# Two query columns of the linear memory moved into a seven-product unit, two heads' delays changed, first weights in two transfers

## The chip, the cores and the metric

The kernel runs on one core of one Trainium2 chip. The metric is device time in microseconds (us) for one launch, the median of repeated runs. The profile is one further execution, recorded instruction by instruction. Its engines are PE (matrix products), ACT and DVE (element-wise work, ACT with function tables), POOL (element-wise work and DMAs that accumulate) and SP (DMA issues). PEld is the weight load that belongs to each matmul.

## The reference

One layer of a streaming encoder on 512 prompt tokens and 64 tokens of a running stream, width 1024, in float32:

```python
h = layer_norm(ALPHA * x + 0.5 * swiglu_ffn(x, ffn1_w_gu, ffn1_w_down))
q, k, v, o, i, f, a_q, a_k, a_v, g_ml, g_att = split(h @ w_in)
qk, new_conv = silu(causal_dwconv(concat([q, k]))), last 3 rows of (history, q, k)
# linear memory ("mLSTM"): 4 heads of 256, chunked, with states C, n, m
y_ml  = (norm(mlstm(q, k / 16, v, i, f)) * g * sigmoid(o)) @ w_ml_proj
y_att = band_attention(a_q, a_k, a_v) @ w_att_proj          # 16 heads of 64
h = layer_norm(ALPHA * h + (sigmoid(g_ml) * y_ml + sigmoid(g_att) * y_att) @ w_out)
y = layer_norm(ALPHA * h + 0.5 * swiglu_ffn(h, ffn2_w_gu, ffn2_w_down))
```

`w_in` is a block of 1024-row columns of 128 outputs each: columns 0 to 7 are q of the linear memory (two for each head: 0 and 1 for head 0, 4 and 5 for head 2), 8 to 15 its k, 16 to 23 v, 24 to 31 o; 32 to 55 are attention q, k, v, and 56 to 71 the two gates. The queries and keys of the linear memory pass a causal convolution over four tokens and a SiLU before they are used.

## The kernel before

All activations lie feature-major, 128 features by 576 tokens a tile. Each float32 operand is split in a high part and a low remainder (`wh`, `wl` for weights; hi, lo for activations), and each product is three matmuls: wh·hi, wh·lo, wl·hi. ACT makes `wh` and DVE `wl`; for the columns in the set `ADDED`, `wl` comes instead from ACT (the negated high part) and an accumulating POOL DMA that reads the weights again.

The stages, by the times of the profile: the first feed-forward block until about 405 us; the columns of `w_in` for v, o, most gates and attention v as *units* (about 435 to 585 us); attention with its q and k columns (until about 780); the attention projection (until 850); the linear memory, heads 0 to 3 (850 to about 1043); two projections; the second feed-forward block (1160 to 1548).

Two kinds of product occur. A plain column (`gemm`) takes 8 feature tiles by 3 matmuls by two halves of the tokens, 256 and 320 wide: 48 matmuls. A unit (`Units`, `Columns`) makes a 2-by-2 block, two columns by two halves of 288 tokens, in seven products rather than eight (the Strassen-Winograd scheme): 7 products by 4 feature tiles by 3 matmuls are 84 matmuls, 288 wide. It needs sums of weight tiles on DVE and ACT, and sums of activation tiles (`Combos`), made once in each stage that has units: `Combos.make` splits eight sums, each with the hi part on ACT and the lo part as an ACT pass (times -1) and an accumulating POOL DMA (`add_lo`). `Columns` writes the outputs to two tiles of 576 tokens, and a `keep` function stores these off chip.

The order on PE is written by hand. `od.now` is a clock that each matmul moves on by a nominal time; `later(dt, fn)` puts a piece of work on a heap, and `od.tick()`, called between feature tiles of the plain columns, places each piece that has come due between them. The orders of ACT, DVE, POOL and SP are set by the framework's scheduler from priorities and dependences. Every engine runs its list in order.

In the linear memory a head has these pieces. `ml_kq`: two k columns, then two q columns; `conv_start` copies a column's result out of its bank to the tile `R` on ACT, `conv_rest` runs four DVE passes over `R` to `U`, SiLU on ACT to `qf` and the split (`qk` for the queries). `turn5` turns keys (`qf`) and values (`vf`, loaded from off chip) by five transposes; the sinks write `kwh`, `vh` on ACT and `kwl`, `vl` on DVE. `ml_decay` makes `Mb` and the decay tiles `D` by Exp on ACT; SiLU and Exp lie in different function tables, so an ACT_TABLE_LOAD stands before each change. `weights(b)` multiplies q with k (`aux<-qk,s`) and scales by `D` to `W`; `state(e)` multiplies k with v (`aux<-vh,kwh`) to `cn`, `cs`; `hidden(b)` multiplies `W` with v (`aux<-vh,W`). Each of these pieces has its own delay after the head's k or q columns. The pieces of a head come due during the columns of the next.

At the start eight transfers are under way at once; later ones wait for one of them. The first three weight columns come in k-pairs of feature tiles: gate 0 and gate 1 in one transfer, up 0 in another. `ones_r` is a constant made on ACT.

Of the kernel before, what the change touches and what calls it, by code (L numbers as in the profile page):

```python
# [17 lines left out]
P = 128  # L18
# [68 lines left out]
def tile_layer(ctx: ExitStack, tc: tile.TileContext, ins, outs):  # L87
# [37 lines left out]
    def f(ap):  # L125
        return ap.bitcast(F32)
# [305 lines left out]
    def plan_in(cols_):  # L432
        for c in cols_:
            plan.append((("in", c), w_in[c]))
# [10 lines left out]
        a, b = ins["w_ap"][j], ins["w_ap"][j + 1]  # L445
        plan += [(("dsap", j, x), w) for x, w in (("a", a), ("u", b), ("t", None), ("b", b[:, :512]))]
    for h in range(4):
        plan_in((8 + 2 * h, 9 + 2 * h, 2 * h, 2 * h + 1, *FILL[h]))
    plan_in((63,))
    plan += [(("mp", j), ins["w_mp"][j]) for j in range(KT)]  # L450
    plan += [(("o", j), ins["w_o"][j]) for j in range(KT)]
# [19 lines left out]

    for k0 in range(0, KT, 2):
        ww = slice(k0 * P, (k0 + 2) * P)
        SP.dma_start(w0[:, 0:3:2, ww], ins["w_gu1"][0:2, :, ww].rearrange("c p n -> p c n"))
        load_x(0, k0, ACT if k0 < 4 else SP)
        SP.dma_start(w0[:, 1, ww], ins["w_gu1"][FT, :, ww])
    for k0 in range(0, KT, 2):
        load_x(1, k0, SP)
    cols = const.tile([P, NCOL], F32, name="cols")
# [38 lines left out]
                    prev = split_x(0, k0 + c)  # L518
    for k in range(KT):
        split_x(1, k)  # L520
    act(ones_r, one_, scale=1.0 / P)
    first.close()


# [246 lines left out]
    class Combos:  # L771
# [876 lines left out]
    KEEP = {48: keep_a, 16: keep_v, 24: keep_o, 56: keep_g, 64: keep_g}  # L1648
    pairs = [(c, b) for c in range(0, KT, 2) for b in (16, 24)] + [(0, 56), (6, 64), (2, 48), (4, 48), (6, 48)]
# [178 lines left out]
    hp = hstack.enter_context(tc.tile_pool(name="hp", bufs=8, reuse_waits="tile"))  # L1828
    HF = []
    mstack = ExitStack()  # L1830
    mp = mstack.enter_context(tc.tile_pool(name="ml", bufs=1, reuse_waits="tile"))
    conv_st = mp.tile([P, 16, 6], F32, name="conv_st")
    vh, vl = (mp.tile([P, 5, 258], F32R, name=s) for s in ("vh", "vl"))
# [32 lines left out]
    def conv_rest(ct, scale, room, tail=None):  # L1866
# [31 lines left out]
    hid, states, backs, order = [0], [0], [0], {}  # L1898

    def ml_kq(h):  # L1900

# [18 lines left out]
        for e in range(2):  # L1920
# [9 lines left out]
            def v_turn(vf, sink):  # L1930

                if hid[0] < 5 * h:
                    later(300, lambda: v_turn(vf, sink))
                else:
                    turn5(vf, sink)

            later(7500 + 6500 * e, lambda vf=vf, s=v_sink, fn=v_turn: fn(vf, s))
        ml_decay(h, st)
        qtail = mp.tile([P, 2, NS], F32, tag="qtail", name=nm("qtail"))
        for e in range(2):  # L1940
            ct = 2 * h + e
            cb = conv_start(ct)
            gemm(one(("in", ct)), H, [cb])
            _, hi, lo = conv_rest(ct, 1.0, lambda: slot(F32R, mp, "qk", bufs=4), qtail[:, e, :])
            st["q"].append((hi, lo))
        st["qtail"] = qtail
        return st

# [39 lines left out]
    def ml_early(h, st):  # L1988
# [33 lines left out]

        for b in range(5):

            later(10000 + 2100 * b if h == 3 else 11000 + 2600 * b, lambda b=b: weights(b))

    def ml_late(h, st):
        W, (c0, ch, cl), wdb, qs_ = st["W"], st["C"], st["wdb"], st["qs"]
# [20 lines left out]

        def hidden(b):  # L2050

            assert backs[0] == 2 * h
            ps = bank()
            if b < 4:
                w = P
# [226 lines left out]
```

## Time and profile before

| what | value |
|---|---|
| three runs | 1551.35, 1549.96 and 1551.93 us, median 1551.35 |
| the profiled execution | 1550.32 us, its span 1548.6 us, granted clock 0.999 |
| PE busy in the span | 1532.1 us, 99% |
| DVE, ACT, POOL busy | 1163.7 us (75%), 884.1 us (57%), 198.5 us (13%) |

The 1.7 us between the profiled time and its span lie before the first and after the last instruction. Times of the trace count from the span's start. A row of the timeline gives start, duration, engine, line, operation, tiles written and read, shape and count, and in brackets the idle time before it with what ended it. Rows of one form that follow each other are put together; their durations then overlap, since the engines start an instruction before the last has left. So what one instruction costs in a queue is the distance from its start to the next one's start. The 48 matmuls of a plain column write a bank named `mm`, attention and memory pieces a bank named `aux`.

### The profile page before, as it was taken

The numbers are of one execution on the slowest core, as the hardware profiler recorded it, in microseconds if no ns is written. First come the engines' busy times: TensorE is split into PE (matmuls) and PEld (weight loads), VectorE is DVE, ScalarE is ACT, GpSimd is POOL, SyncE is SP. The second block draws the span as 40 slices with busy tenths as digits, with TensorE's granted clock in tenths as the row PEclk, the third lists the DMA queues.
The fourth block names the chain that finished last, engine by engine and source line by source line (L and its number), as shares of the span: only waits on it lengthen the run. The fifth ranks groups of instructions, "written<-read, shape, count | busy, mean of one in ns | idle before, by whom it ended". The sixth has DMA issues, their size and how long they took to land.

```text
span 1548.6 us, 29509 instructions
## 1 busy us (share of the span) xinstructions
PE 1532.1 (99%) x11587; PEld 1516.3 (98%) x11587; DVE 1163.7 (75%) x2256; ACT 884.1 (57%) x1672; POOL 198.5 (13%) x372
## 2 busy tenths in 40 slices
PE   9999999999999999999999999999999999999998
PEld 9999999999999999999999999999999999999997
DVE  7877778756999767887677577765779878787756
ACT  7545446533766557776864777753456454557323
POOL 2000000100200015544300311102120000001000
PEclk9999999999999999999999999999999999999999
DMA  9322223534544448676634965542653323217244
GB/s 258 113 100 92 94 98 103 129 107 148 174 149 147 151 171 228 160 181 156 141 99 146 278 147 138 121 141 83 200 122 104 109 82 110 82 64 192 81 128 150
DMA packets 80259, 211.93 MB, mean 137 GB/s; under 512 B 9080, under 2 KB 20984, under 8 KB 80120
## 3 DMA queue, kind: packets, MB, share of 16 engines
q1 hardware_dynamic: 66072, 172.29, 33.9%
q0 software_dynamic: 12896, 36.05, 13.3%
q8 instruction: 91, 1.49, 0.4%
q10 hardware_dynamic: 1152, 1.70, 0.3%
q14 instruction: 48, 0.39, 0.1%
HBM read 174.82 MB, written 22.22 MB: 127 GB/s over the span
## 4 chain that ended last, share of the span: by engine, by line
PE 45%; DVE 3%; ACT 3%; issue 1%; DMA 0%; POOL 0%; DVEq 0%; ACTq 0%; POOLq 0%
PE mm L133 35%; PE aux L133 8%; PE aux L143 1%; DVE U L153 1%; DVE s L153 1%; ACT L147 0%; DMA wr<-in_w_ap 0%; ACT wh L147 0%; ACT sc L147 0%; DVE o L150 0%; DVE wl L150 0%; DVE s L150 0%; ACT R L147 0%; ACT qf L147 0%; ACT s L147 0%
## 5 line engine op out<-in xcount | busy, mean ns | idle before, releaser
L133 PE MATMUL mm<-s,wh 128*128 128x288 f32 (+2 forms) x3430 | 700.9, 298 | 1.1 <-DVE s L150 0.4
L133 PEld LDWEIGHTS mm<-s,wh 128*128 128x128 f32 x3430 | 548.7, 189 | 4.2 <-DVE s L150 1.5
L133 PE MATMUL mm<-s,wl 128*128 128x288 f32 (+2 forms) x1705 | 503.2, 295 | 0.0
L133 PEld LDWEIGHTS mm<-s,wl 128*128 128x128 f32 x1705 | 321.1, 188 | 0.2 <-DVE wl L150 0.2
L147 ACT ACTIVATE wh<-wr 128x1024 fp32r<-128x1024 f32 (+2 forms) x136 | 133.0, 979 | 144.6 <-PE mm L133 85.5
L133 PE MATMUL mm<-tx,wh 128*128 128x288 f32 x778 | 158.4, 296 | 0.0
L150 DVE TENSOR_TENSOR wl<-wr,wh 128x1024 fp32r<-128x1024 f32 (+2 forms) x97 | 108.8, 1125 | 56.9 <-ACT wh L147 56.8
L133 PEld LDWEIGHTS mm<-tx,wh 128*128 128x128 f32 x778 | 124.9, 188 | 0.0
L133 PE MATMUL mm<-tx,wl 128*128 128x288 f32 x383 | 113.0, 295 | 0.6 <-DVE wl L150 0.6
L916 ACT ACTIVATE wh<-wt 128x1024 fp32r<-128x1024 f32 x53 | 56.2, 1060 | 88.4 <-DVE wt L150 88.4
L150 DVE TENSOR_TENSOR wl<-wt,wh 128x1024 fp32r<-128x1024 f32 x53 | 64.8, 1222 | 53.9 <-ACT wh L916 52.7
L133 PE MATMUL mm<-h,wh 128*128 128x256 f32 (+2 forms) x384 | 78.3, 295 | 0.0
L150 DVE TENSOR_TENSOR wl<-wu,wh 128x1024 fp32r<-128x1024 f32 x50 | 61.2, 1223 | 22.1 <-ACT wh L916 22.1
L197 POOL DMA_DIRECT2D s<-s x16 | 13.7, 855 | 491.4 <-ACT s L147 252.2
L133 PEld LDWEIGHTS mm<-tx,wl 128*128 128x128 f32 x383 | 72.0, 188 | 0.9 <-DVE wl L150 0.9
L916 ACT ACTIVATE wh<-wu 128x1024 fp32r<-128x1024 f32 x50 | 52.9, 1058 | 32.7 <-PE mm L133 32.5
L147 ACT ACTIVATE h<-h 128x288 f32<-128x288 f32 x80 | 35.0, 437 | 64.1 <-DVE h L150 64.0
L150 DVE TENSOR_TENSOR wl<-ws,wh 128x1024 fp32r<-128x1024 f32 x53 | 64.6, 1219 | 0.4 <-ACT wh L916 0.3
L150 DVE TENSOR_TENSOR ws<-wu 128x1024 f32<-128x1024 f32 x53 | 64.3, 1214 | 0.0
L133 PEld LDWEIGHTS mm<-h,wh 128*128 128x128 f32 x384 | 61.5, 188 | 0.2
L916 ACT ACTIVATE ah<-wu 128x512 fp32r<-128x512 f32 x53 | 33.4, 631 | 44.6 <-PE mm L133 41.3
L133 PE MATMUL mm<-h,wl 128*128 128x256 f32 (+2 forms) x192 | 56.5, 294 | 0.0
(397 smaller groups left out, 3622.0 us busy)
## 6 DMA issues: line engine op xcount, KB each, us to landing
wu<-in_w_gu SPq DMA_DIRECT2D x80, 512.0 KB, 4.3
wr<-in_w_in SPq DMA_DIRECT2D x46, 512.0 KB, 4.1
wr<-in_w_dn SPq DMA_DIRECT2D x40, 512.0 KB, 3.5
wl<-in_w_in POOLq DMA_DIRECT2D x38, 512.0 KB, 7.0
wu<-in_w_in SPq DMA_DIRECT2D x26, 512.0 KB, 4.5
wr<-in_w_dn SPq DMA_DIRECT2D x20, 384.0 KB, 3.4
s<-s POOLq DMA_DIRECT2D x16, 288.0 KB, 3.6
wr<-in_w_ap SPq DMA_DIRECT2D x8, 512.0 KB, 3.5
```

What stands on the lines that cost most here:

```text
L133: PE.matmul(out, lhsT, rhs, start=start, stop=stop, **kw)
L143: PE.transpose(out, in_, idn)
L147: return ACT.activation(out, in_, func, **kw)
L150: return (eng or DVE).tensor_tensor(out, a, b, op=op)
L153: return DVE.scalar_tensor_tensor(out=out, in0=a, scalar=s, in1=b, op0=op0, op1=op1)
L197: return POOL.dma_start(lo, src, accum_op=ALU.add)
L916: self.last = ACT.activation(hi, src, AF.Copy)
```

## The change

1. **A fourteenth unit.** Columns 1 and 5 (the second query column of heads 0 and 2) become one unit behind the thirteen. `keep_q` stores its two tiles off chip (`QD`). Heads 0 and 2 no longer have these two plain columns: three remain in each.
2. **The pieces of heads 0 and 2.** `conv_load` fetches the stored column into a tile `RQ` by two SP transfers and makes the two small POOL copies; the rest of the convolution runs on `RQ` rather than `R`, 1000 nominal ns after the decays. The delays of heads 0 and 2 change: the second turn of v from 14000 to 12000, `weights` from 11000 + 2600b to 13000 + 2600b, `state` from 5500 + 1800e to 9000 + 1800e, `hidden` from 19500 + 2200b to 21000 + 2200b. `state` is put back by 300 while not both turns of v have been placed.
3. **The start.** The first k-pair of gate 0 and gate 1 comes in two transfers, gate 0 first, then up 0, then gate 1. `ones_r` is made behind the splits of the first tokens.
4. **`Combos.make`.** Of the eight lo parts, those of n = 0 with i = 2, 3 are a DVE subtraction rather than ACT and a POOL DMA.

```diff
-        plan_in((8 + 2 * h, 9 + 2 * h, 2 * h, 2 * h + 1, *FILL[h]))
+        plan_in((8 + 2 * h, 9 + 2 * h, 2 * h, *((2 * h + 1,) if h in (1, 3) else ()), *FILL[h]))
...
-        SP.dma_start(w0[:, 0:3:2, ww], ins["w_gu1"][0:2, :, ww].rearrange("c p n -> p c n"))
+        if k0:
+            SP.dma_start(w0[:, 0:3:2, ww], ins["w_gu1"][0:2, :, ww].rearrange("c p n -> p c n"))
+        else:
+            SP.dma_start(w0[:, 0, ww], ins["w_gu1"][0, :, ww])
         load_x(0, k0, ACT if k0 < 4 else SP)
         SP.dma_start(w0[:, 1, ww], ins["w_gu1"][FT, :, ww])
+        if not k0:
+            SP.dma_start(w0[:, 2, ww], ins["w_gu1"][1, :, ww])
...
-    act(ones_r, one_, scale=1.0 / P)
+    with tc.issue_after(prev.ins):
+        act(ones_r, one_, scale=1.0 / P)
...
-                        self.added = add_lo(lo, hi, t)
+                        if n or i < 2:
+                            add_lo(lo, hi, t)
+                        else:
+                            tt(lo, t, f(hi), ALU.subtract)
...
+    QD = {c: away("qd") for c in (1, 5)}
+
+    def keep_q(c, tiles):
+        for e in range(2):
+            SP.dma_start(QD[c + 4 * e], tiles[e])
...
-    pairs = [...] + [(0, 56), (6, 64), (2, 48), (4, 48), (6, 48)]
-    un = Columns([(b + c, b + c + 1) for c, b in pairs],
+    pairs = [...] + [(0, 56), (6, 64), (2, 48), (4, 48), (6, 48), (1, 0)]
+    un = Columns([(b + c, b + c + (1 if b else 4)) for c, b in pairs],
...
+    RQ = rqp.tile([P, LR], F32, name="RQ")
+    POOL.memset(RQ[:, 0:3], 0.0)
...
+    def conv_load(ct):
+        DVE.tensor_copy(RQ[:, 515:518], cols[:, C_HIST + 3 * ct:C_HIST + 3 * ct + 3])
+        SP.dma_start(RQ[:, 3:515], QD[ct][:, 0:NP_])
+        SP.dma_start(RQ[:, 518:582], QD[ct][:, NP_:])
+        POOL.tensor_copy(conv_st[:, ct, 0:3], RQ[:, 512:515])
+        POOL.tensor_copy(conv_st[:, ct, 3:6], RQ[:, 579:582])
...
-            later(7500 + 6500 * e, lambda vf=vf, s=v_sink, fn=v_turn: fn(vf, s))
+            later(7500 + (6500 if h in (1, 3) else 4500) * e, lambda vf=vf, s=v_sink, fn=v_turn: fn(vf, s))
...
-        for e in range(2):
+        if h in (0, 2):
+            conv_load(2 * h + 1)
+            later(1000, lambda: st.update(q1=conv_rest(2 * h + 1, 1.0, room, qtail[:, 1, :], RQ)[1:]))
+        for e in range(1 if h in (0, 2) else 2):
...
-            later(10000 + 2100 * b if h == 3 else 11000 + 2600 * b, lambda b=b: weights(b))
+            later(10000 + 2100 * b if h == 3 else (11000 if h == 1 else 13000) + 2600 * b, lambda b=b: weights(b))
...
         def state(e):
+            if vts[0] < 2 * h + 2:
+                later(300, lambda: state(e))
+                return
...
-            later(5500 + 1800 * e, lambda e=e: state(e))
+            later((5500 if h in (1, 3) else 9000) + 1800 * e, lambda e=e: state(e))
...
-            later(16000 + 1800 * b if h == 3 else 19500 + 2200 * b, lambda b=b: hidden(b))
+            later(16000 + 1800 * b if h == 3 else (19500 if h == 1 else 21000) + 2200 * b, lambda b=b: hidden(b))
```

Two places show what this does to the engines' lists. Both are ACT's. The first is the head of its list, behind its first four transfers (`w` is the tile of the first three weight columns, `s` on the right the raw tokens). Before:

```order
L147 ACT_TABLE_LOAD
L147 ACTIVATE ones_r<-one 128x128
L514 ACTIVATE wh_99<-w_90 128x256
L503 ACTIVATE s_71<-s_91 128x256
L514 ACTIVATE wh_101<-w_90 128x256
L503 ACTIVATE s_73<-s_92 128x256
L514 ACTIVATE wh_103<-w_90 128x256
```

And in the changed kernel:

```order
L519 ACT_TABLE_LOAD
L519 ACTIVATE wh_99<-w_90 128x256
L508 ACTIVATE s_71<-s_91 128x256
L519 ACTIVATE wh_101<-w_90 128x256
L508 ACTIVATE s_73<-s_92 128x256
L519 ACTIVATE wh_103<-w_90 128x256
```

The pass for `ones_r` is gone from ahead of the first weights; in SP's list the first transfer (128x2x256 before) is now 128x256, and every transfer from the second k-pair on stands one place later. The second place is its list in head 0 of the linear memory, around the second turn of v, whose result `vh` (128x4x128, then 64x128) the state products need. Before:

```order
L147 ACTIVATE kwh<-aux_11143,tcol 128x128
L147 ACTIVATE kwh<-aux_11156,tcol 64x128
L147 ACTIVATE wl_11194<-wh_11193 128x1024
L147 ACTIVATE R<-mm_11079 128x256
L147 ACTIVATE R<-mm_11126 128x256
L147 ACTIVATE R<-mm_11126 128x64
L147 ACTIVATE kwh<-aux_11143,tcol 128x128
L147 ACTIVATE vh<-aux_11200 128x4x128
L147 ACTIVATE vh<-aux_11207 64x128
L147 ACTIVATE kwh<-aux_11143,tcol 128x128
L147 ACT_TABLE_LOAD
L147 ACTIVATE qf_11074<-U_11069 128x512
```

And in the changed kernel, where the stored column's SiLU (`qf`) comes ahead and the first decays `D` stand between:

```order
L147 ACTIVATE vh<-aux_11255 64x128
L147 ACTIVATE qf_11128<-U_11123 128x512
L147 ACTIVATE qf_11128<-U_11123 128x64
L147 ACT_TABLE_LOAD
L147 ACTIVATE D_11194<-Mb_11088,tcol 64x64
L147 ACTIVATE qk_11129<-qf_11128 128x576
L147 ACTIVATE kwh<-aux_11295,tcol 128x128
L147 ACTIVATE kwh<-aux_11308,tcol 64x128
L147 ACTIVATE D_11197<-Mb_11088,tcol 128x512
L147 ACTIVATE kwh<-aux_11295,tcol 128x128
L147 ACTIVATE vh<-aux_11315 128x4x128
L147 ACTIVATE vh<-aux_11322 64x128
```

The second `vh` now stands behind the table load, two decays and the stored column's SiLU and split. On PE 39 matmuls of plain columns stood between the second turn of v and the first state product, and now 21; from the first state product to the first of `weights(0)` there were 51 matmuls, and now 42.

More of the change, by code (lines that the diff above doesn't have):

```diff
@@ L1646, in keep_a @@
             SP.dma_start(outs["v"][:, c + e, :], tiles[e])
-    KEEP = {48: keep_a, 16: keep_v, 24: keep_o, 56: keep_g, 64: keep_g}
-    pairs = [(c, b) for c in range(0, KT, 2) for b in (16, 24)] + [(0, 56), (6, 64), (2, 48), (4, 48), (6, 48)]
-    un = Columns([(b + c, b + c + 1) for c, b in pairs],
+    KEEP = {0: keep_q, 48: keep_a, 16: keep_v, 24: keep_o, 56: keep_g, 64: keep_g}
+    pairs = [(c, b) for c in range(0, KT, 2) for b in (16, 24)] + [(0, 56), (6, 64), (2, 48), (4, 48), (6, 48), (1, 0)]
+    un = Columns([(b + c, b + c + (1 if b else 4)) for c, b in pairs],
                  [lambda tiles, c=c, fn=KEEP[b]: fn(c, tiles) for c, b in pairs],
@@ L1830, in tile_layer @@
     mstack = ExitStack()
+    rqp = mstack.enter_context(tc.tile_pool(name="rq", bufs=1, side="right", reuse_waits="tile"))
     mp = mstack.enter_context(tc.tile_pool(name="ml", bufs=1, reuse_waits="tile"))
@@ L1864, in conv_start, with conv_rest @@
         return cb
-    def conv_rest(ct, scale, room, tail=None):
+    def conv_load(ct):
[4 more added lines that the diff above has]
+        POOL.tensor_copy(conv_st[:, ct, 3:6], RQ[:, 579:582])
+    def conv_rest(ct, scale, room, tail=None, R=R):
         U = mp.tile([P, LU], F32, tag="U", name=nm("U"))
@@ L1896, in turn5 @@
                 sink(b0, nb, w, ps[:w, :nb * P].rearrange("p (b c) -> p b c", c=P))
-    hid, states, backs, order = [0], [0], [0], {}
+    hid, states, backs, vts, order = [0], [0], [0], [0], {}
     def ml_kq(h):
@@ L1935, in v_turn @@
                     turn5(vf, sink)
-            later(7500 + 6500 * e, lambda vf=vf, s=v_sink, fn=v_turn: fn(vf, s))
+                    vts[0] += 1
+            later(7500 + (6500 if h in (1, 3) else 4500) * e, lambda vf=vf, s=v_sink, fn=v_turn: fn(vf, s))
         ml_decay(h, st)
         qtail = mp.tile([P, 2, NS], F32, tag="qtail", name=nm("qtail"))
-        for e in range(2):
+        room = lambda: slot(F32R, mp, "qk", bufs=4)
+        if h in (0, 2):
+            conv_load(2 * h + 1)
+            later(1000, lambda: st.update(q1=conv_rest(2 * h + 1, 1.0, room, qtail[:, 1, :], RQ)[1:]))
+        for e in range(1 if h in (0, 2) else 2):
             ct = 2 * h + e
@@ L1943, in ml_kq @@
             gemm(one(("in", ct)), H, [cb])
-            _, hi, lo = conv_rest(ct, 1.0, lambda: slot(F32R, mp, "qk", bufs=4), qtail[:, e, :])
-            st["q"].append((hi, lo))
+            st["q"].append(conv_rest(ct, 1.0, room, qtail[:, e, :])[1:])
+        if h in (0, 2):
+            st["q"].append(st["q1"])
         st["qtail"] = qtail
@@ L2050, in hidden @@
         def hidden(b):
-            assert backs[0] == 2 * h
+            assert backs[0] == 2 * h and vts[0] == 2 * h + 2
             ps = bank()
```

## The prediction

> **What bounds the kernel now.** I read the busy times of the page first, then the chain that ended last, then windows by stage, and last the timelines of the two places where the lists change.
>
> ```profile
> PE 1532.1 (99%) x11587; PEld 1516.3 (98%) x11587; DVE 1163.7 (75%) x2256; ACT 884.1 (57%) x1672; POOL 198.5 (13%) x372
> ```
>
> PE is the bound nearly everywhere: 16.5 us of the span of 1548.6 are all the idle time it has. So a change can win in two ways, fewer or shorter matmuls, or some of those gaps; and it can lose by new gaps. The chain in the second feed-forward stage, made of units alone, gives the price of a unit's matmul:
>
> ```profile
> 1198.22 201.08 PE mm L133 x1518
> ```
>
> That is 132.5 ns for each 288-wide matmul. The windows below hold the units of `w_in` (the first), the first two plain columns of the linear memory (the second: 96 matmuls of the columns, and two records at its edges), the pieces of head 0, and heads 1 to 3. The columns are the window, its length, the busy time with the count of PE, PEld, DVE, ACT and POOL, PE's granted clock, the DMA share and GB/s.
>
> ```profile
> 435.00:585.00 150.00, 149.21 (x1123) 148.44 (x1122) 122.10 (x170) 87.47 (x135) 7.73 (x11) 1.00 0.47 157
> 850.17:862.97 12.80, 12.80 (x98) 12.80 (x97) 4.50 (x11) 6.90 (x9) 6.35 (x19) 1.00 0.94 263
> 862.97:911.00 48.03, 47.63 (x363) 46.34 (x362) 32.55 (x74) 41.07 (x94) 10.10 (x25) 1.00 0.88 226
> 911.00:1043.00 132.00, 132.00 (x1024) 130.66 (x1023) 97.56 (x250) 90.54 (x203) 21.76 (x56) 1.00 0.53 134
> ```
>
> Two things are to be seen. Two plain columns cost 12.80 us without a gap. And in head 0 (third row) ACT is busy for 41.07 of 48.03 us, 86%, where in heads 1 to 3 it is 69%: head 0 is the one place of this stage where ACT is short of time, and it is the place whose list changes most.
>
> **The matmuls: -1.67.** The unit costs 84 x 132.5 ns = 11.13 us. The two plain columns that go cost 12.80 us. PE's own work falls by 1.67 us. The Trainium skill ("TensorE: Matmul & The Clock Gate", Back-to-back issue gap) gives N/2.4 + 2.5 ns for an isolated warm matmul. By that the saving would be estimated at 48 x (109.2 + 135.8) - 84 x 122.5 ns = 1.47 us; the rows give more for each matmul, and the measured ones stand in the sum.
>
> **The unit beside PE: 0 (0 to +0.5).** It brings the sums of weight tiles on DVE and ACT. The first window shows what covers them: about 13 units in 150 us with PE busy for 149.21, so DVE at 81% and ACT at 58% leave 0.79 us of idle time in all, 0.06 a unit. Its own work goes at that same rate. Its four weight tiles of 512 KB and the two stores of 288 KB meet a DMA share of 0.47. In exchange heads 0 and 2 lose their plain column's load, its accumulating transfer and its passes; each gains 288 KB of loads. In head 0 that relieves a DMA share of 0.88 to 0.94. I take 0; as upper bound, nearly the idle time of the whole window once more.
>
> **The start: -0.1, and `Combos.make`: -0.3 (together -0.7 to +0.5).** Timelines of ACT, PE and SP at the start, and the loads' sizes with the median time from issue to landing:
>
> ```profile
> 2.76 1.28 ACT L147 ACT_TABLE_LOAD   x1 [2.76 <-issue]
> 4.05 0.31 ACT L147 ACTIVATE ones_r<-one 128x128 fp32r<-128x128 f32 x1
> 4.31 0.42 ACT L514 ACTIVATE wh<-w 128x256 fp32r<-128x256 f32 x1
> 7.26 0.42 ACT L514 ACTIVATE wh<-w 128x256 fp32r<-128x256 f32 x1 [1.22 <-DMA w<-in_w_gu]
> 5.08 0.97 PE L133 MATMUL mm<-s,wh 128*128 128x256 f32 x2 [0.23 <-ACT s L503]
> 2.31 0.47 SPq L476 DMA_DIRECT2D w<-in_w_gu  x1
> 3.92 0.38 SPq L474 DMA_DIRECT2D w<-in_w_gu  x1
> w<-in_w_gu SPq DMA_DIRECT2D x4, 256.0 KB, 4.8
> ...
> w<-in_w_gu SPq DMA_DIRECT2D x4, 128.0 KB, 3.8
> ```
>
> Without `ones_r`, and with half the bytes in the first transfer, the first pass can start at 4.05 rather than 4.31, and PE's first product at 4.82 rather than 5.08. But at 7.26 ACT waited 1.22 us for the second k-pair of weights, and the bytes ahead of that pair are the same as before. PE then has 0.26 us more to wait there. So nearly all of it is given back; I keep 0.1. The bad end is the queue: SP stood still from 2.78 to 3.92, since a ninth transfer waits for one of the eight in flight. After the change the ninth is the second pair's up column (issued at 2.31 before), now at about 3.9. With 3.8 us to land it is there at 7.7, and ACT wants it behind the pass of 7.26, at about 7.9: 0.2 to spare.
>
> Later in the same stage the combined sums are made, and PE has one stall:
>
> ```profile
> 33.16 0.68 ACT L147 ACTIVATE s<-s 128x576 fp32r<-128x576 f32 x1
> 34.30 1.05 ACT L916 ACTIVATE wh<-wu 128x1024 fp32r<-128x1024 f32 x1
> 35.38 1.22 DVE L150 TENSOR_TENSOR wl<-wu,wh 128x1024 fp32r<-128x1024 f32 x1 [0.47 <-ACT wh L916]
> 36.66 0.40 PE L133 MATMUL aux<-s,wl 128*128 128x288 f32 x1 [0.73 <-DVE wl L150]
> ```
>
> PE waited 0.73 us for `wl`, which waited for ACT's `wh`, which stood behind the negating pass of 33.16 (0.68, of which about 0.1 overlaps the next). By the changed list that pass is one of those that go, and DVE gets a subtraction of 576 in its stead (0.76, by the 576-wide pass in the next fence). ACT brings `wh` about 0.6 earlier, but DVE has only its idle 0.47 there to take up the 0.76, so the new pass holds `wl` back by about 0.3: I take 0.3 back of the 0.73. In the other two stages that make such sums, PE shows no such wait, and I take nothing.
>
> **Head 0 of the linear memory: +2.3 (-0.6 to +4.5).** ACT, then DVE, then PE, around the second turn of v, the state products and `weights(0)`; the last row is `weights(0)` of head 1:
>
> ```profile
> 870.58 0.38 ACT L147 ACTIVATE R<-mm 128x256 f32<-128x256 f32 x1 [1.35 <-DVE U L153]
> ...
> 876.64 1.31 ACT L147 ACTIVATE D<-Mb,tcol 128x384 f32<-128x384 f32 x3
> 877.84 0.64 ACT L147 ACTIVATE ch<-c 128x516 fp32r<-128x516 f32 x1
> 878.37 1.06 ACT L147 ACTIVATE wh<-wr 128x1024 fp32r<-128x1024 f32 x1
> ...
> 880.76 0.77 ACT L147 ACTIVATE R<-mm 128x256 f32<-128x256 f32 x3
> 881.39 0.39 ACT L147 ACTIVATE kwh<-aux,tcol 128x128 fp32r<-128x128 f32 x1
> 881.63 0.78 ACT L147 ACTIVATE vh<-aux 128x512 fp32r<-128x512 f32 x2
> ...
> 882.68 1.28 ACT L147 ACT_TABLE_LOAD   x1
> 883.98 0.63 ACT L147 ACTIVATE qf<-U 128x512 f32<-128x512 f32 x1
> ...
> 889.23 0.77 ACT L147 ACTIVATE qf<-U 128x512 f32<-128x512 f32 x2
> 890.03 0.69 ACT L147 ACTIVATE qk<-qf 128x576 fp32r<-128x576 f32 x1
> 882.29 0.69 DVE L150 TENSOR_TENSOR vl<-aux,vh 128x512 fp32r<-128x512 f32 x1
> 890.75 0.76 DVE L153 SCALAR_TENSOR_TENSOR qk<-qf,qk 128x576 fp32r<-128x576 f32 x1 [0.19 <-ACT qk L147]
> 878.34 0.71 PE L143 MATMUL aux<-ident,vf 128*128 128x128 f32 x5
> 878.80 0.48 PE L133 MATMUL mm<-s,wh 128*128 128x256 f32 x2
> 884.03 0.28 PE L133 MATMUL aux<-vh,kwh 128*128 128x258 f32 x1
> 890.31 1.09 PE L133 MATMUL aux<-qk,s 128*128 128x512 f32 x4
> 891.57 0.73 PE L133 MATMUL aux<-qk,s 128*128 128x512 f32 x2 [0.16 <-DVE qk L153]
> 901.97 0.77 PE L143 MATMUL aux<-ident,qf 128*128 128x128 f32 x5 [0.19 <-ACT Mb L147]
> 932.20 1.57 PE L133 MATMUL aux<-qk,s 128*128 128x512 f32 x6
> ```
>
> Before, ACT worked without a pause from 870.58 to the second `vh` at 881.63: 28 instructions in 11.05 us. DVE's `vl` ended at 882.98, and the state products came at 884.03, so they had 1.05 us to spare. In the changed list 24 instructions stand between the same two points. Gone from there are three decays (1.20, to the start of `ch`), `ch` (0.53) and three `R` copies (0.63); new are the stored column's SiLU and split (about 0.7 and 0.6, from 889.23 and 890.03 less the overlap). That is 11.05 - 2.36 + 1.3 = 9.99 us, so `vh` starts at 880.57. `vl` starts 0.66 us behind it and takes 0.69: 881.9, and 882.1 if DVE has part of another pass before it.
>
> PE comes much earlier. Counted by its list, the second turn of v stands 1.24 us earlier, at 877.10. The turn takes 0.46, and the 21 matmuls that remain take 21 x 0.134 = 2.82 (39 of them took 5.23, from 878.80 to 884.03). So PE is at the first state product at 880.38, 3.65 earlier than before, where ACT is 1.06 earlier. It waits until 882.1: **+1.7**.
>
> `weights(0)` follows. 42 matmuls (30 of 0.12, 12 of 0.134) bring PE there at 887.3. The stored query column is the second that `weights(0)` reads; the plain one, which is late, is the first. Its split stands in ACT's list behind the last `vh`, three decays, two `kwh`, `ch`, three `R`, a table load, two SiLU passes and a `cn`, which add up to 5.75 us by the distances of their starts (the dearest in the rows above: 1.30 for the table load, 1.20 for the decays). So hi runs from 886.3 to 887.0, and DVE's lo takes 0.76, at once or behind up to 0.8 of a pass of the convolution: 887.8 to 888.6. The second matmul needs it. I take 888.5, near the late end, since DVE's row before shows such a pass ahead of the first lo: **+1.2**.
>
> Before, `weights(0)` took from 890.31 to 892.30, 1.99 us, where head 1's took 1.57; and PE lost 0.19 at 901.97. PE comes later to both pieces relative to what they wait for, and I count these 0.6 as gone: 1.7 + 1.2 - 0.6 = **+2.3**. The low end is that ACT and DVE clear both in time and the 0.6 go. The high end has 2.5 and 2.0 at the two places, and nothing gone.
>
> The rest costs nothing, each by a cover. The `RQ` transfers of head 0 are issued about 9 us ahead of the first pass over them, and loads took 3.8 to 4.8 us at the crowded start. POOL's two copies of head 2's `RQ` stand ahead of head 0's masks on `D`, which only `weights(0)` wants. Where `hidden` comes later, PE has columns to fill in. Heads 1 to 3 lose no time before (132.00 of 132.00 in the windows), and ACT at 69% there has room for head 2's moved pieces.
>
> **The sum.** -1.67 + 0 - 0.4 + 2.3 = +0.2 on the profiled 1550.32 us: 1550.5. That execution lies 1.03 below the median of the runs, so against the median I give **1551.5**: no change, since less than 0.2%, 3.1 us, can hardly be told from none here.
>
> **The rivals.**
> *The gain comes through.* ACT or DVE reach `vh` and the late query a good 2 us sooner than my sum, for instance since passes that I put in sequence overlap. For it: ACT's list there waited for nothing, so whatever it is spared shows at once. Then -1.67 - 0.4 + 0 = -2.1, 1549.3: still within 0.2%.
> *Faster.* The same, the old gaps go too (-0.6), and so does the whole stall ahead of 36.66 (-0.4 more): -3.1, 1548.2, just at the bound. Against it: it needs three covers to hold at once.
> *Slower.* One mechanism: the stored column's SiLU, its split and the table loads stand ahead of `vh` in ACT's in-order list, in head 2 as in head 0. If head 2 waits as head 0 does (2 x 2.3) and one of the two runs to the high end (+2.2), the sum is -2.1 + 6.8 = +4.7: 1556.1. It decides from 5.2 us of such waits. Against it: ACT at 69%, not 86%, behind head 0.
> *The split start loses.* A transfer of 128 KB that is issued into full queues takes longer than the 3.8 us; at 5.1 (the 256 KB ones took 4.8) the second pair's up column lands at 9.0, 1.1 us after ACT wants it: +1.1 instead of -0.1, so 1552.7. The Trainium skill ("DMA: Bandwidth & Descriptors", on measured sizes) has the rule to batch transfers to 1 MiB or more, as small ones carry a fixed cost; by that, splitting one of 256 KB is a loss. The row of 128 KB with 3.8 us, behind the 256 KB with 4.8, has the small one landing sooner, and that weakens it.
>
> **Chances.** The waits eat the gain: 0.46. The gain comes through: 0.27. Faster by more than 0.2%: 0.13. Slower by more: 0.10. The start loses: 0.04, within 0.2%. So faster 0.13, same 0.77, slower 0.10. For the range I add the ends: -1.67 - 0.7 - 0.6 = -3.0 on the one side and -1.67 + 0.5 + 0.5 + 4.5 = +3.8 on the other; on the median 1548.4 and 1555.2. A tenth of the chance lies beyond each or near it, so I draw the upper in and the lower out a little: 1548.0 to 1554.6.
>
> **What would show it.** The timeline of PE in head 0 should have a gap of 1 to 2.5 us ahead of the first `aux<-vh,kwh` with DVE's `vl` as its end, and one of about 1 us at the second `aux<-qk,s`. The window of `w_in`'s units should be 11.1 us longer with less than 1 us of idle time. The first product should start near 4.8, and the one at 36.66 wait less. I am wrong if PE's waits in head 0 come to less than 1 us in all, if head 2 shows any above 0.5, or if the attention stage, whose PE list is the same as before, changes by over 1 us.

## The result, and the profile after

The changed kernel is slower: 1560.79 us median of six runs (1558.30 to 1564.29) against 1551.10 us for the kernel before in the same comparison. The ratio is 1.0065, with an interval of 1.0055 to 1.0076. The forecast was 1551.5, no change, with a range of 1548.0 to 1554.6. The profiled execution, the quickest of the six, took 1558.30 us, with a span of 1556.2. The page's row of engines:

```profile
PE 1532.6 (98%) x11575; PEld 1514.6 (97%) x11575; DVE 1172.1 (75%) x2268; ACT 884.1 (57%) x1668; POOL 198.2 (13%) x369
```

The windows by stage, with the columns of the windows of before (the unit stage; head 0 of the linear memory; head 1; heads 2 and 3):

```profile
435.00:585.00 150.00, 149.86 (x1125) 149.23 (x1126) 121.97 (x166) 84.74 (x132) 1.97 (x2) 1.00 0.44 149
...
863.00:911.00 48.00, 43.76 (x322) 42.12 (x321) 29.72 (x66) 37.37 (x81) 15.31 (x42) 1.00 0.91 264
911.00:960.00 49.00, 47.47 (x370) 46.34 (x370) 35.98 (x93) 34.46 (x82) 9.68 (x22) 1.00 0.60 135
960.00:1043.00 83.00, 81.29 (x627) 79.65 (x626) 60.74 (x164) 55.53 (x124) 13.82 (x34) 1.00 0.43 106
```

The unit stage is as full as before. The linear memory is not: PE idles 4.2 us in head 0's window, 1.5 in head 1's and 1.7 in the last two heads', where the kernel before had 0.4 and nothing. The waits of PE in this stage, first of the kernel before and then of the changed one (what waits, for which engine's tile, us in total, times, longest):

```profile
PE aux L143 <- ACT Mb L147: 0.2, 1, 0.2
PE aux L133 <- DVE qk L153: 0.2, 1, 0.2
```

```profile
PE aux L133 <- DVE qk L153: 2.4, 2, 1.4
PE aux L143 <- DVE kwl L153: 2.0, 1, 2.0
PE aux L143 <- DVE vl L150: 1.2, 2, 0.9
PE aux L133 <- ACT qk L147: 0.5, 1, 0.5
PE aux L133 <- ACT vh L147: 0.5, 1, 0.5
PE aux L133 <- DVE vl L150: 0.3, 1, 0.3
...
```

The times in the list are idle time alone. A second measure takes in the pipeline's refill: the distance from each matmul's start to the next, less the usual distance for its width (119 ns at 256, 133 at 288, 147 at 320), summed where more than 0.06 us is left. I call these gaps. Over the whole span they come to 31.4 us before and 40.6 after. The difference of 9.2, less the 1.6 to 1.7 us of matmuls saved, is 7.6, and the spans differ by 7.6 (1556.2 - 1548.6). So the gaps and the saved matmuls account for the whole change of this trace. By place, counted from the first column of the linear memory:

| place | before | after | forecast |
|---|---|---|---|
| first 50 us | 5.0 | 4.4 | -0.4 |
| rest ahead of the linear memory | 20.0 | 20.9 | 0 |
| head 0, turn of k (26 us in) | 0.2 | 2.2 | 0 |
| head 0, state products (32) | 0 | 1.2 | +1.7 |
| head 0, first weights product (39), 1.7 of it at one matmul | 0.4 | 1.9 | +1.2 |
| head 0, later | 0.4 | 0 | gone |
| head 1, first weights product (81) | 0 | 2.0 | 0 |
| head 2, turns of k and v (103, 105) | 0 | 1.5 | 0 |
| heads 2 and 3, later (144, 158) | 0 | 0.8 | 0 |

The lists of the start did what was expected. PE's first product starts at 4.78 us rather than 5.08. The second k-pair came earlier too (6.76 rather than 7.26). DVE starts `wl` at 34.77 rather than 35.38, and the gap of 0.9 at 36.66 is 0.3 here. The gaps of the start differ between traces, though: in the sixteen traces of this document that have the new start, those of the first 50 us come to 3.8 to 6.4, and in seven of them the one near 36.66 is again 0.9 to 1.2. So the fall from 5.0 to 4.4 is not told from none. Of these rows of the changed kernel the first is PE's, the second ACT's, the others DVE's:

```profile
4.78 0.87 PE L133 MATMUL mm<-s,wh 128*128 128x256 f32 x2
6.76 0.42 ACT L519 ACTIVATE wh<-w 128x256 fp32r<-128x256 f32 x1 [0.94 <-DMA w<-in_w_gu]
34.10 0.75 DVE L150 TENSOR_TENSOR s<-h,s 128x576 fp32r<-128x576 f32 x1
34.77 1.22 DVE L150 TENSOR_TENSOR wl<-wu,wh 128x1024 fp32r<-128x1024 f32 x1
```

The largest gap that I had not forecast is the one at the turn of k. These are the rows of the changed kernel around it: SP issues `RQ`'s load, POOL copies from it, DVE makes the first pass over it and the last `kwl` of the first turn, and PE goes on:

```profile
872.63 0.45 SPq L1887 DMA_DIRECT2D RQ<-qd  x1
884.76 0.19 POOL L1889 COPY conv_st<-RQ 128x3 f32<-128x3 f32 x1 [7.33 <-DMA RQ<-qd]
885.05 0.58 DVE L157 TENSOR_SCALAR U<-RQ,cols 128x579 f32<-128x579 f32 x1 [3.07 <-POOL conv_st L1889]
889.61 0.35 DVE L153 SCALAR_TENSOR_TENSOR kwl<-aux,tcol,kwh 128x128 fp32r<-128x128 f32 x1
890.02 0.30 PE L143 MATMUL aux<-ident,qf 128*64 128x128 f32 x1 [2.01 <-DVE kwl L153]
```

`RQ` was issued at 872.63 and had landed at 884.76, 12.1 us later. DVE stood for 3.07 us at its first pass over `RQ`, with `kwl` behind it in its list, and a transpose waited 2.01 us for the bank that the last `kwl` reads. Head 2's load, issued at 889.58, took 8.6 us. From there on both DVE and ACT have no time left; the windows are those around the state products, before and after:

```profile
872.00:890.00 18.00, 17.95 (x141) 17.71 (x140) 13.01 (x29) 16.74 (x38) 5.71 (x12) 1.00 0.97 274
```

```profile
885.00:898.00 13.00, 10.18 (x76) 9.42 (x75) 12.68 (x29) 12.03 (x30) 4.26 (x7) 1.00 1.03 318
```

DVE was busy for 72% there and is now at 98%, ACT stays at 93%, and PE fell from 100% to 78%.

### The profile page after: what moved, and what is told of

Its sections match the earlier page's. It is cut to its first block, busy times and chain, and to the rows that moved or that the text cites. A ratio compares the mean times of both kernels' runs of the same rounds, so it can differ in the third digit from the quotient of the medians.

```text
span 1556.2 us, 29501 instructions
## 1 busy us (share of the span) xinstructions
PE 1532.6 (98%) x11575; PEld 1514.6 (97%) x11575; DVE 1172.1 (75%) x2268; ACT 884.1 (57%) x1668; POOL 198.2 (13%) x369
## 4 chain that ended last, share of the span: by engine, by line
PE 43%; DVE 4%; DMA 3%; ACT 2%; issue 1%; POOL 0%; DVEq 0%; SPq 0%; ACTq 0%
PE mm L133 34%; PE aux L133 8%; DMA wr<-in_w_in 1%; PE aux L143 1%; DVE U L153 1%; DMA RQ<-qd 1%; DMA wr<-in_w_ap 1%; DVE o L150 0%; DVE s L153 0%; ACT sc L147 0%; ACT L147 0%; DVE wl L150 0%; DMA og<-od 0%; ACT wh L147 0%; DVE s L150 0%
## 5 line engine op out<-in xcount | busy, mean ns | idle before, releaser
L133 PE MATMUL mm<-s,wh 128*128 128x288 f32 (+2 forms) x3395 | 693.7, 298 | 0.4 <-DVE s L150 0.2
L133 PEld LDWEIGHTS mm<-s,wh 128*128 128x128 f32 x3395 | 542.8, 189 | 3.2 <-DVE s L150 0.9
L133 PE MATMUL mm<-s,wl 128*128 128x288 f32 (+2 forms) x1688 | 498.2, 295 | 0.0
L133 PEld LDWEIGHTS mm<-s,wl 128*128 128x128 f32 x1688 | 317.9, 188 | 0.2 <-DVE wl L150 0.2
L133 PE MATMUL mm<-tx,wh 128*128 128x288 f32 x797 | 162.3, 296 | 0.0
L925 ACT ACTIVATE wh<-ws 128x1024 fp32r<-128x1024 f32 x54 | 56.9, 1053 | 0.7 <-PE mm L133 0.4
```

What stands on the lines that cost most here:

```text
L133: PE.matmul(out, lhsT, rhs, start=start, stop=stop, **kw)
L925: self.last = ACT.activation(hi, src, AF.Copy)
```

## The experiments

The theories have letters in the expectations. A is the prediction's (ACT's list in head 0: table load, decays and the stored column's passes ahead of v). L says that the `RQ` loads land late. O says that the order of ACT's and DVE's lists, against less time on PE, is what costs. All ratios are against the kernel before, with their intervals.

**The start alone.** The kernel before with points 3 and 4 of the change.

> The kernel before with two parts of the change alone: the first weights in two transfers with ones_r behind the splits, and the two lo parts on DVE. The prediction's sum for these is -0.4 us, and the trace of the changed kernel has 0.6 us less of PE's gaps in the first 50 us. So 1550.5 to 1551 beside 1551.1. If these parts cost something after all, it is above 1551.5.

1550.82 us, ratio 1.0000 (0.9991 to 1.0009). Its gaps in the first 50 us are 4.2 rather than 5.0, within the scatter given above. No cost shows; a gain or a loss of 0.4 lies within what this comparison can tell. The loss of 9.7 us is not here.

**`RQ` loaded first.**

```diff
+    conv_load(1)
     for h in range(4):
         st = ml_kq(h)      # head 0 without its own conv_load
```

> The changed kernel with head 0's load of RQ issued ahead of its v, o and C0 loads. Theory L (landing): RQ took 12.1 us to land and DVE's list stood behind the first pass over it, so PE's 2.2 us gap at the turn of k goes and the state products' gap shrinks: 2 to 3 us faster than the changed kernel, near 1558. Theory A (ACT's list, the one of the prediction): the gap only moves to the state products, at most 0.5 us faster.

1561.96 us, 1.0069 (1.0054 to 1.0084): not faster, and the gap at the turn of k is still there, at 2.4 us. `RQ` did land in time (POOL copied from it at 875.48), but the third weight column was late, and ACT's list stood behind it. SP's issues of that column (the first of two) and of `RQ`, and ACT's pass over the column:

```profile
866.21 3.07 SPq L266 DMA_DIRECT2D wr<-in_w_in  x2
869.34 0.54 SPq L1887 DMA_DIRECT2D RQ<-qd  x1
873.76 1.06 ACT L147 ACTIVATE wh<-wr 128x1024 fp32r<-128x1024 f32 x1 [3.46 <-DMA wr<-in_w_in]
```

The copies for the convolutions stand behind that pass, so the convolutions were 3.3 us late, counted from the first column of the linear memory. The weight load had been issued ahead of `RQ`, 1.3 us later in the stage than in the changed kernel, and ACT used it 7.5 us after its issue rather than 5.6. So `RQ` can account for a part of its lateness at most, and a later expectation that takes `RQ` to have stood ahead of it is not borne out by SP's list. This run does not test L cleanly, since a weight load was late as well.

**POOL's copies of head 2's `RQ` behind the masks.**

```diff
+        with tc.issue_after(order["sel"].ins) if "sel" in order else nullcontext():
             POOL.tensor_copy(conv_st[:, ct, 0:3], RQ[:, 512:515])
             POOL.tensor_copy(conv_st[:, ct, 3:6], RQ[:, 579:582])
```

> The changed kernel with POOL's two copies of head 2's RQ behind the masks of heads 0 and 1 (on POOL only). Theory L: the masks on D and the copy of the query's tail no longer wait for a load that lands 8.6 us after its issue, and the gap of 1.9 us within head 0's first weights product shrinks to 0.8 or less: 1 to 1.5 us faster, near 1559.5. Theory A: that gap is set by the split of the plain query column on ACT, and nothing changes.

1559.32 us, 1.0052 (1.0036 to 1.0069). The gap at the one matmul of the weights product is 1.4 us (1.7 in the changed kernel), not the 0.8 of L. The median is 1.5 lower than the changed kernel's, but the two intervals overlap; this part of L is not shown.

**The o-gate loads later.**

```diff
+            with tc.issue_after(wst["load"].ins) if h else nullcontext():
                 SP.dma_start(st["og"][e], OD[2 * h + e])
```

> The changed kernel with the o-gate loads of heads 1 to 3 (six of 288 KB) held behind the weight loads of their own head in SP's list. Theory L, with the load on the DMA engines as its cause (a share of 0.91 in 863 to 911 us): both RQ loads land earlier by some 3 to 5 us, and the run is 2 to 4 us faster than the changed kernel, 1557 to 1559, with less spread between executions. Theory A: no change, and the RQ loads' landing may move without an effect on the time.

1562.14 us, 1.0072 (1.0057 to 1.0087): not faster. `RQ` was issued at 873.1 and was there at 885.9. The six transfers were behind it in the queue, and to take them away did not bring it forward; what stood ahead of it did not change.

**No load of `RQ`.**

```diff
-        SP.dma_start(RQ[:, 3:515], QD[ct][:, 0:NP_])
-        SP.dma_start(RQ[:, 518:582], QD[ct][:, NP_:])
...
-    POOL.memset(RQ[:, 0:3], 0.0)
+    POOL.memset(RQ, 0.0)
```

> The changed kernel without the loads of RQ (the tile is set to zero once by POOL, so the second query column of heads 0 and 2 is not the real one; all other work stays). Theory L (the late loads): the 2.2 us gap at the turn of k and about 1 us of the gap in head 0's weights product go, 3 us or more faster than the changed kernel's 1560.8, so 1556 to 1558. Theory O (the order of ACT's and DVE's lists, with four convolutions per head in less PE time): the waits stay behind other entries of the lists, and it is within 1.5 us of the changed kernel; the gaps of heads 1 and 2 (1.95 and 1.5 us, the same to 0.02 us in four kernels) stay in any case.

1556.92 us, 1.0035 (1.0022 to 1.0048), 3.9 us below the changed kernel. This kernel leaves the load out, so what it computes is not the layer. The gap at the turn of k is gone, while that of the weights product stays at 1.5 and heads 1 and 2 keep 1.98 and 1.54. So the wait for `RQ` causes the first and little or nothing of the others.

**The stored column behind the plain one.**

```diff
-            later(1000, lambda: st.update(q1=conv_rest(...RQ)[1:]))
...
+            with tc.issue_after(order["u"].ins):      # the last pass over U of the plain query column
+                st["q"].append(conv_rest(2 * h + 1, 1.0, room, qtail[:, 1, :], RQ)[1:])
```

> The changed kernel with the convolution of the stored column held behind that of the plain query column in DVE's list, in heads 0 and 2. Theory O: the first pass over RQ no longer stands ahead of kwl in DVE's list, so the 2.2 us gap at the turn of k goes, and v's remainders come earlier; but the stored column's split is then late for the weights product. Net 1 to 3 us faster than the changed kernel, if that product waits less than 2 us more. Theory L says the same for head 0, so this run does not tell L and O apart; it tells whether the place of the stored column in the list is what costs.

1564.43 us, 1.0088 (1.0073 to 1.0104): not faster. The median is 3.6 above the changed kernel's, though the intervals just overlap. The gap at the turn of k shrinks to 0.3 as O has it, but the state products wait 2.35, the weights product 2.5, and head 2's turn 2.5. The place in DVE's list moves the wait; it does not remove it.

**The delays of before, with the unit; the new delays, without it.** Two kernels: the changed one with all delays as before, and the kernel before with the new start, the two lo parts and the new delays.

> The changed kernel with the delays of the kernel before in heads 0 and 2. Each piece comes due 1.5 to 3.5 us earlier on PE than in the changed kernel, while ACT and DVE make its inputs no sooner. If the gaps are inputs that PE outruns (theories L and O), it is slower than the changed kernel by 3 us or more: above 1563. If the new delays themselves are at fault, it is faster.

1560.38 us, 1.0063 (1.0045 to 1.0082), the changed kernel's time; both expectations fail. In its trace head 1 has no gap, but head 0 has 4.7 us of them and head 2 3.7: they sit elsewhere and come to nearly the same sum.

> The kernel before with the new start, the two lo parts on DVE and the new delays of heads 0 and 2, but without the unit: the two query columns stay plain. If the delays and the moved v turn cost by themselves (through the lists of ACT and DVE that follow from them), it is 2 us or more above 1551. If the loss comes from the columns' shorter time on PE against the same work on ACT and DVE, it is within 1 us of 1551.

1555.65 us, 1.0032 (1.0020 to 1.0045): 4.8 us of loss without the unit. The waits of its linear memory:

```profile
PE aux L143 <- DVE kwl L153: 2.9, 1, 2.9
PE aux L133 <- DVE D L150: 1.1, 1, 1.1
...
```

The first stands in head 1, whose delays had not been touched. So a change of head 0's and head 2's delays alone gives new lists for ACT and DVE, with a wait of 2.9 us in another head. It costs by itself, and it is not the whole: with the unit and the old delays the loss is 9.5 us.

**`RQ` ahead of `C0` and of the o-gates, behind the third weight load.**

```diff
+        if h == 0:
+            conv_load(1)            # ahead of ml_decay, which loads C0
...
-            SP.dma_start(st["og"][e], OD[2 * h + e])
...
+        with tc.issue_after(wst["load"].ins):       # behind the query columns
+            for e in range(2):
+                SP.dma_start(st["og"][e], OD[2 * h + e])
```

> The changed kernel with head 0's RQ load ahead of C0 and of all o-gate loads, and behind the third weight load (in the earlier run it stood ahead of it, and the weights came 4 us late); each head's o-gate loads follow its query columns. Theory L: RQ lands in time for its place in DVE's list (21 us into the stage rather than 23), the 2.2 us gap at the turn of k goes as it did without the load: 2.5 to 4 us faster than the changed kernel, near 1557. If the DMA engines were simply full, some other load is late in its stead and the time stays near 1560.

1558.67 us, 1.0049 (1.0032 to 1.0066). The gap at the turn of k is gone, as without the load, and no other load took its place. `RQ` still took 11.1 us, but it was issued sooner and landed 20.6 us into the stage rather than 23.0. The other gaps stay: 1.2, 1.5, 2.0 and 1.5. Its median is 2.1 below the changed kernel's, though the intervals overlap; what is shown is the gap in the trace. L holds, then, for that one gap, if the load is placed where it displaces none that is needed sooner.

**Head 1's split ahead of the next weights.**

```diff
+            order["qk"] = act(hi, q, scale=scale)
...
+  with tc.issue_after(order["qk"].ins) if plan[c][0] == ("in", 15) else nullcontext():
       act(hi[:, a:a + step], raw[:, a:a + step])
```

> The changed kernel with one weight column's passes (the second k column of head 3) held behind the split of head 1's last query column in ACT's list. In the kernel before that split stood ahead of the next weight column's passes; in the changed one wh (0.95 us), the rest of R and wl (0.95 us) stand ahead of it. Theory O: head 1's gap of 1.95 us within weights(0) goes and nothing else moves: 1.5 to 2 us faster, near 1559, and the trace shows the gap below 0.3. Theory L: the gap stays.

1557.65 us, 1.0045 (1.0030 to 1.0060), 3.1 below the changed kernel, though the intervals just overlap. Head 1's gap is gone altogether. ACT's rows there, of the changed kernel and of this one:

```profile
938.24 0.39 ACT L147 ACTIVATE cn<-aux 128x258 f32<-128x258 f32 x1 [3.00 <-PE aux L133]
938.89 1.06 ACT L147 ACTIVATE wh<-wr 128x1024 fp32r<-128x1024 f32 x1 [0.26 <-PE mm L133]
...
941.43 1.08 ACT L147 ACTIVATE wl<-wh 128x1024 fp32r<-128x1024 f32 x1
942.38 0.70 ACT L147 ACTIVATE qk<-qf 128x576 fp32r<-128x576 f32 x1
```

```profile
940.25 0.39 ACT L147 ACTIVATE cn<-aux 128x258 f32<-128x258 f32 x1 [3.00 <-PE aux L133]
941.15 0.78 ACT L147 ACTIVATE R<-mm 128x256 f32<-128x256 f32 x3 [0.51 <-DVE U L153]
941.79 0.79 ACT L147 ACTIVATE qf<-U 128x512 f32<-128x512 f32 x2
942.62 0.69 ACT L147 ACTIVATE qk<-qf 128x576 fp32r<-128x576 f32 x1
```

From `cn` to the query's split `qk` it was 4.14 us, with `wh` and `wl` of a column that PE needs three columns later between them; it is 2.37 now. This cause of head 1's loss is shown. (In this profile head 0's gap at the turn of k was 3.5, not 2.2: `RQ` landed 24.4 us into the stage. PE's clock then ran at half for 6.8 us, which the last section takes up.)

**The mends together.** The two before, with head 2's turns of v due later (11500 and 14500); and with head 0's `state` and `weights` due 2 and 1 us later besides.

> The two mends above together, and head 2's turns of v placed 2 us later (due at 11500 and 14500 instead of 7500 and 12000), since ACT reaches v only behind the stored column's SiLU, a table load and a decay there. Theory O with L: the gaps of 2.2, 1.95 and 1.5 us go, -5 to -6 us against the changed kernel: 1555. If one gap moves rather than goes, 1557 or more.

> The three mends, and head 0's state and weights products due 2 and 1 us later, so that PE does plain columns (21 and 12 matmuls more or less) while ACT and DVE finish v and the late query. The two gaps that the prediction named (1.2 and 1.7 us) should shrink by about 2 in sum: 1553, against 1551 before. If the inputs only come later still, it equals the run with three mends.

1554.65 us, 1.0025 (1.0016 to 1.0034), and 1553.41 us, 1.0018 (1.0009 to 1.0028). Six of the ten us are back. Head 2's gap did not go: with v's turns later, PE waits 1.05 and 0.7 us there for `kwl` and `vl`. Later products in head 0 moved its waits to other places as well, and the two kernels are not told apart by their intervals.

**The decays behind v.**

```diff
-        later(6000, decays)
+        later(9000 if h in (0, 2) else 6000, decays)
```

> The changed kernel with the decays of heads 0 and 2 due 3 us later, which puts the Exp table load and all decays behind v and behind the late query's split in ACT's list. If the cause of the prediction holds (1.30 us of table load and 0.87 of decays ahead of v), the gap of 1.2 us at head 0's state products goes, and that of 1.7 within weights(0) falls below 0.8, since the late query's SiLU needs no second table load ahead of it. The gap at the turn of k (2.2) stays, as does head 1's. So 2 to 3 us faster than the changed kernel, 1558. If they do not move, v's own turn or DVE sets them.

1561.46 us, 1.0071 (1.0056 to 1.0087): no gain. The gap at the state products shrinks only from 1.2 to 0.8, that of the weights product (its one matmul) from 1.7 to 1.3, and two of 0.6 to 0.7 appear behind it. ACT reaches v no sooner without the table load ahead, since it now waits for DVE:

```profile
893.50 0.37 ACT L147 ACTIVATE kwh<-aux,tcol 128x128 fp32r<-128x128 f32 x1 [1.47 <-DVE kwl L153]
893.76 0.74 ACT L147 ACTIVATE vh<-aux 128x512 fp32r<-128x512 f32 x2
```

`vh` starts at 893.76, and at 893.89 in the changed kernel. Theory A named a part of the list that is there, but not the one that sets the end: ACT stands for `kwl` on DVE. That DVE and ACT are both full is read from the windows above; no run gave DVE less to do there.

> The three mends and the decays of heads 0 and 2 behind v. The three mends stood at 1554.65, with gaps in the stage of 4.4 us: 1.2 and 1.5 in head 0 and 1.75 in head 2. If the decays ahead of v cause all of these, 3 to 4 us go: 1550.5 to 1551.5, level with the kernel before, and PE's own work, 2 us less by unit and start, is what remains as a gain over it of 0 to 1 us.

> The same with head 0's state and weights products due 2 and 1 us later. If the decays behind v clear the gaps already, this changes nothing (within 1 us of the run before); if a part of them is left, it is up to 1 us faster.

1553.54 us, 1.0017 (1.0009 to 1.0026), and 1554.64 us, 1.0024 (1.0015 to 1.0033). Neither beats the kernel before, and the forecast of 1550.5 to 1551.5 fails: the waits moved again. Against the three mends, the first has 0.5 rather than 1.5 in the weights product, but 1.3 rather than 0.2 at the turn of k, and two new gaps of 0.6 to 0.7 behind. Over the linear memory its gaps come to 8.5, where those of the three mends come to 7.3.

## Why the prediction was wrong, point by point

- **The matmuls, -1.67: right.** With the gaps of 9.2 us taken off, the span is 1.6 us shorter, and the same sum fits the other profiles (with the three mends: gaps +4.3, less 1.6, is +2.7, and the span is 3.0 longer; delays alone, without the unit: gaps +7.7, of which 2.6 are matmuls at half clock, and the span is 7.5 longer). The unit's side work was covered: 0.14 us of idle time in 435 to 585 us. It loads two weight tiles of 512 KB, not the four of the prediction (`wu<-in_w_in` goes from 26 to 28), which changes no term.
- **The start, -0.4: the lists moved as forecast, a gain is not shown.** Gaps there fell by 0.6 in this trace, less than they differ among traces with the same start. Against the rival that the split start loses: the second pair was taken up 0.5 us sooner, not later. The rule in the Trainium skill ("DMA: Bandwidth & Descriptors", on measured sizes) that small transfers waste bandwidth shows no cost here (1.0000 with the start alone).
- **Head 0's state and weights products, +1.7 and +1.2, old gaps gone: the sizes were about right, the cause in part wrong.** Measured were 1.2 and 1.9, and the old 0.4 at the later turn went. I had put them down to ACT's list. Freeing ACT of the table load and the decays took 0.4 off each and gained nothing in sum, since other waits took their place. DVE is 98% busy there, so ACT and DVE together are the likely bound. That the sizes came out near is in part luck.
- **"The `RQ` transfers of head 0 are issued about 9 us ahead ... and loads took 3.8 to 4.8 us": this step failed,** for 2.0 us. The load took 12.1. I had priced it by loads at the crowded start, though the trace of before has the same kind of load in the very stage. These are two rows of its list of DMA issues from 838 to 901 us, the last number the median time to landing:

```profile
og<-od SPq DMA_DIRECT2D x8, 288.0 KB, 13.0
...
vf<-vd SPq DMA_DIRECT2D x4, 288.0 KB, 7.9
```

  With 8 to 13 us against the 9 us of lead, the load could be late, and DVE's pass over it stood ahead of `kwl`.
- **"Heads 1 to 3 lose no time before, and ACT at 69% there has room": this step failed,** for 4.3 us. A mean share says nothing about what stands ahead of what. The changed lists of these heads were there to be read; I read only head 0's. In head 1 they put a weight column's passes ahead of the query's split, which cost 2.0 us and went when that order was mended.
- **The rival "slower"** had the right direction and head 2 as a second place, but it was too small (its high case was +4.7 us on the profiled execution, where +8.0 was measured), its mechanism was too narrow, and I gave it 0.10.
- **PE's clock: a term that the prediction did not have.** The profiled execution shows 8.0 of the 9.7 us between the medians, and its clock was full over the linear memory. Traces of kernels with nearly the same lists hold stretches at half clock behind long waits, which cost 1.2 to 1.7 us each (last section). The clocks of the changed kernel's six executions fit that: 0.998 in the two shortest, 0.996 to 0.997 in the other four, where one such stretch takes 0.001 off the mean. So the rest of the loss is likely there, but no trace of the changed kernel itself shows it.

Open: what makes head 2's gap of 1.5 us. In its trace ACT reaches v's first turn behind the stored column's SiLU, a table load and a decay. But v due later (1.75) and the decays behind v (1.5) both left as much or more, so this cause is read from the lists and not shown. That POOL waits for head 2's `RQ` ahead of the masks is in the trace; that it costs time isn't shown either.

## What to carry to other kernels

Where PE has no idle time, other engines may still be without slack, stage by stage: a cut of PE's work in such a stage can be paid back as waits when the work of the engines that feed it doesn't fall too. Here 6.4 us of matmuls left each of two heads, and the four convolutions, the turns and the decays stayed. When an order of one engine is changed by hand and a scheduler makes the others', read the new lists at every place that waits for them, not only where the edit is. And price a transfer by the landing times of its own stage.

## What the runs showed of the hardware that was not expected

A load of 256 KB took 8.6 to 12.1 us to land with the DMA share at 0.91 (264 GB/s) in 863 to 911 us, against 3.8 us for 128 KB at the start (346 GB/s in 4 to 6 us). To take away 1.7 MB behind it in the queue changed nothing. Issued ahead of `vf`, the o-gates and `C0` it took about 6 us. Ahead of the o-gates and `C0` alone, with `vf` and a weight load just before it, it took 11.1.

In 8 of the 17 traces PE's granted clock falls to half in the midst of the work, for 3.41 us, once for twice as long. These are the two stretches of the kernel with POOL's copies behind the masks; the third number from the end is the clock:

```profile
892.43:895.84 3.41, 3.41 (x15) 3.33 (x16) 3.41 (x10) 3.38 (x8) 0.80 (x3) 0.50 1.04 329
947.04:950.45 3.41, 3.41 (x16) 3.24 (x16) 2.63 (x5) 1.98 (x4) 0.00 (x0) 0.50 0.98 164
```

In such a stretch a 256-wide matmul starts every 213 ns rather than 119, and a 320-wide every 267 rather than 147; that adds 1.2 to 1.7 us. The first one here follows a wait of 2.43 us at the turn of k, the second the waits of head 1's weights product. The stretches of a trace lie whole multiples of 3.41 us apart. With each trace cut into cells of that length from the start of its clock record, all nine cells of the linear memory that hold 1.95 us or more of gaps are followed by a cell at half clock, and none that holds 1.88 or less is, but for the second half of the long stretch. At the end of the attention stage cells with about 1.5 us were followed by one in three traces and not in others, so the bound is not the same everywhere. A wait can thus cost more than its own length, and whether it does hangs on where it falls among the cells.
